# Matmuls in groups of two wide and two narrow, a fixed issue order on TensorE and a second column pair that runs one unit late

## The chip, the cores and the metric

The kernel runs on one core of a Trainium2 chip. The metric is device time in microseconds (us) of one execution. The kernel before takes 2563.12 us, the median of three runs (2562.52 to 2567.24).

## The reference: what is computed

A trunk of two pre-norm residual layers over 256 tokens of width 2048, each a token mixer followed by a gated feed-forward block, with a last RMSNorm. All inputs and outputs are float32.

```python
def ssd_mixer(u, w_in, conv_w, conv_b, dt_bias, a_log, d_skip, norm_w, w_out):   # layer 0
    z, xbc, dt_raw = split(u @ w_in)              # 2048 -> 4096 + 6144 + 64
    xbc = silu(causal_dwconv(xbc, conv_w, conv_b))
    y = ssd_chunked(...) + xh * d_skip            # 64 heads of 64, 8 groups, state 128
    yg = group_rms_norm(y * silu(z)) * norm_w
    return yg @ w_out                             # 4096 -> 2048

def short_conv_mixer(u, w_in, conv_w, w_out):     # layer 1
    bg, cg, h = split(u @ w_in, 3)                # 2048 -> 3 x 2048
    return (bg * causal_dwconv(cg * h, conv_w)) @ w_out

def conv_ffn(u, w_up, conv_w, conv_b, w_down):    # both layers
    g, v = split(causal_dwconv(u @ w_up, conv_w, conv_b), 2)    # 2048 -> 2 x 5632
    return (silu(g) * v) @ w_down                 # 5632 -> 2048

for i in range(2):
    x = x + mixer_i(rms_norm(x, mix_norm_w[i]))
    x = x + conv_ffn(rms_norm(x, ffn_norm_w[i]))
return rms_norm(x, final_norm_w)
```

## The kernel before

**Numbers in two parts.** Every large product is done with values of type float32r. A float32 operand is split into a high part (the value cast to float32r) and a low part (what the cast left out). A weight gives `wh` and `wl`; an activation gives the two halves of one tile `hl`, 256 columns (one per token) of high parts and 256 of low parts. The product of two such operands is taken as high times high, high times low and low times high. With the weight block as the stationary operand, `wh` meets both halves of `hl` in one matmul of 512 columns, which is called a wide product here (line 334 of the kernel before), and `wl` meets the high half in a matmul of 256 columns, a narrow one (line 335). Where the mixer of layer 0 needs the sum at once (`one=True`), the wide product is two narrow ones (lines 331 and 332).

**Units and streams.** A weight unit is 256 rows by 512 columns of a weight matrix. It is loaded by SyncE's queue into one of four `raw` buffers, ScalarE casts it to `wh` (line 287), and VectorE subtracts to get `wl` (line 288); `wh` and `wl` have four buffers each (`WB = 4`). A stream is one call of `stream`: 512 output columns, as two PSUM tiles of two banks (`pts`, the column pairs 0 and 1), accumulated over all units of the contraction (8 units for 2048 rows). For each unit it runs over the four column blocks `t` and over the two 128-row slices `k`. For each `(t, k)` it issues a wide product and then a narrow one, so a unit is eight wide and eight narrow products. `weight_unit` fetches up to `ahead` units beyond the one it returns; `stream` asks for three.

**Behind a stream.** `evac` takes each column pair out of PSUM. In the feed-forward block that is a copy on ScalarE (line 346), a sum and a product with the token's norm factor on VectorE (348, 357), a causal convolution over three positions (one ACTIVATE, line 368, and two SCALAR_TENSOR_TENSOR, line 370, for each of the two blocks), and then, in the gate's streams, a Silu (749), in the value's streams a product with the gate (755) and the split into a new `hl` (212, 213). A residual stream adds PSUM to `x` (698, 700). The PSUM pool `psm` has three such tiles, so that a stream's second tile is the one that the stream before it filled first.

**What sets the order.** The kernel is written in program order, and a scheduler with its own timeline then orders each engine's instructions; only those under `pin` keep their place. So on TensorE the products of two column pairs can change places where the scheduler expects a wait. SyncE's queue carries the weight loads.

**Stages.** The mixer of layer 0 comes first (eight groups of heads, with small matmuls between its streams, and its residual streams), then feed-forward block 0, the mixer of layer 1, and block 1. Block 1's second half differs: activations are stationary and weights move, so that each slice takes three wide products (lines 858 to 860), and the last norm is in token order.

Of the kernel before, what the change touches and what calls it, by code (L numbers as in the profile page):

```python
# [8 lines left out]
F32 = mybir.dt.float32  # L9
# [7 lines left out]
P = 128  # L17
# [22 lines left out]
def trunk_kernel(ctx, tc, a, out):  # L40
# [14 lines left out]
    dpool = ctx.enter_context(tc.tile_pool(name="dpool", bufs=1, space=DRAM))  # L55
    psm = ctx.enter_context(tc.tile_pool(name="psm", bufs=3, space=PSUM))
    psa = ctx.enter_context(tc.tile_pool(name="psa", bufs=2, space=PSUM))

    n_id = [0]

    def uid(s):
        n_id[0] += 1
        return f"{s}_{n_id[0]}"
# [244 lines left out]
    def stream(c0, hls, kcs, evac, one=False, before=None):  # L308

        pts = [psm.tile([P, 2, 512], F32, tag="main", name=uid("main")) for _ in range(2)]
        n = len(kcs)
        put = (lambda ins: ins) if before is None else pin
        for u in range(0, n, KU):
            order = [(t, k) for t in range(4) for k in range(KU)]
            if before is not None and u == 0:
                before(0)
                order.sort(key=lambda tk: tk[1])  # L320
            wh, wl = weight_unit(c0, kcs[u], WB - 1 if before is None else 0)
            for at, (t, k) in enumerate(order):
# [6 lines left out]
                first, last = i == 0, i == n - 1  # L329
                if one:  # L330
                    put(mm(o[:, 0:T], wh[:, k, lw], hl[:, 0:T], start=first, stop=False))  # L331
                    put(mm(o[:, 0:T], wh[:, k, lw], hl[:, T : 2 * T], start=False, stop=False))  # L332
                else:
                    put(mm(o, wh[:, k, lw], hl, start=first, stop=False))  # L334
                put(mm(o[:, 0:T], wl[:, k, lw], hl[:, 0:T], start=False, stop=last))  # L335
        if before is not None:
            before(n // KU)
        if taken[0] < len(plan):
            while len(units) < min(taken[0] + WB - 1, len(plan)):
                load_unit()  # L340
        for p in range(2):
            evac(p, pts[p])
# [345 lines left out]
            hls.append(h)  # L688
        return hls

    def residual_stream(hls, kcs, norm, nhl, nname, one=False):

        for cg in range(D // COLS):

            def evac(p, pt, cg=cg):
                m = 2 * cg + p
                x = xp[m]
                tt(out=x, in0=pt[:, :, 0:T], in1=x, op=ALU.add)
                if not one:
                    tt(out=x, in0=pt[:, :, T : 2 * T], in1=x, op=ALU.add)  # L700
# [39 lines left out]
    def ffn_part(l, part, hls, r):  # L740
        lo, hi = FPARTS[part]
        res = []
        for ch in range(lo, hi, 4):
            gs = []

            def evac_g(p, pt, ch=ch):
                k0 = ch + 2 * p
                y = conv(scaled(pt, r), W_FF, f"fw{l}", NF, k0, f"fb{l}", "g", gpool)
                act(y, y, AF.Silu)
                gs.append(y)  # L750

            def evac_v(p, pt, ch=ch):
                k0 = DFF // P + ch + 2 * p
                y = conv(scaled(pt, r), W_FF, f"fw{l}", NF, k0, f"fb{l}")
                tt(out=y, in0=gs[p], in1=y, op=ALU.mult)
# [11 lines left out]
    for part in range(2):  # L767
        hid = ffn_part(0, part, xhl, r)
        last = part == 1
        residual_stream(  # L770
            hid, range(*FPARTS[part]), norm if last else None, nhl,
            lambda m: ("mix", NKD + 2 * m),
        )


# [6 lines left out]
    for i in range(D // COLS):  # L782
# [21 lines left out]
    residual_stream(  # L804
        yhl, range(NKD), norm, nhl, lambda m: ("ffn", NKD + 2 * m)
    )


# [31 lines left out]
    for part in range(2):  # L840
# [3 lines left out]
        for cg in range(D // COLS):  # L844
# [6 lines left out]
            def products(c, u):  # L851
                wh, wl = held[u]
                for k in range(KU):
# [4 lines left out]
                    mm(pt[:, c, :], hi_, wh[:, k, :], start=(i == 0), stop=False)  # L858
                    mm(pt[:, c, :], hi_, wl[:, k, :], start=False, stop=False)  # L859
                    mm(pt[:, c, :], lo_, wh[:, k, :], start=False, stop=(i == n - 1))  # L860

            def evac(c):
                x = xtok[c][:, cols]
# [49 lines left out]
```

## Time and profile before

| | |
|---|---|
| median of three runs | 2563.12 us |
| the profiled execution | 2563.32 us |
| its span, first to last instruction | 2561.5 us |
| TensorE busy | 2544.6 us, 99% of the span |
| VectorE busy, ScalarE busy | 1790.2 us (70%), 1321.5 us (52%) |
| wide products of streams (line 334) | 5568 |
| narrow products of streams (331, 332, 335) | 768, 768, 6336 |
| wide products of block 1's last part (858 to 860) | 3 x 352 |
| read from HBM | 474 MB, 186 GB/s over the span |

The profiled execution lies 0.2 us above the median, and 1.8 us of it is outside the span. The ends of matmuls are modelled and overlap the next one's start: a wide product has a duration of 396 ns and starts about 230 ns before the next. So rates are read from start to start. "Busy 99%" says that TensorE had a matmul in flight nearly always, and not that it could go no faster.

### The profile page before, as it was taken

What the parts mean: (1) busy time and instruction counts of PE and PEld (TensorE: products, weight loads), DVE (VectorE), ACT (ScalarE), POOL (GpSimd) and SP (SyncE); (2) the same over time, 40 slices, a digit from 0 to 9 for tenths busy, and PEclk for the clock granted to TensorE, in tenths of its full rate; (3) what the DMA queues carried; (4) which work ended last, traced back from release to release, by engine and by line L of the source; (5) the groups of instructions that cost most, each with busy time, mean ns of one, the idle gap of its engine ahead of it and who ended that gap; (6) DMA issues with size and microseconds to landing.
All of it is one profiled execution on the core that took longest, in us unless ns stands there. A gap on an engine that the chain in (4) does not pass through costs nothing.

```text
span 2561.5 us, 38324 instructions
## 1 busy us (share of the span) xinstructions
PE 2544.6 (99%) x15101; PEld 2235.2 (87%) x15101; DVE 1790.2 (70%) x2601; ACT 1321.5 (52%) x1630; POOL 1.1 (0%) x8
## 2 busy tenths in 40 slices
PE   9999999999999999999999999999999999999998
PEld 9999998998888888888888888888888888888886
DVE  7888876788677776557776666666677774577765
ACT  5565643566555554345554444444555553455543
POOL 0000000000000000000000000000000000000000
PEclk9999999999999999999999999999999999999999
DMA  7666655665666665666665666666566666666664
GB/s 229 175 184 193 182 176 188 189 182 172 198 183 191 190 188 181 193 188 183 193 190 181 193 186 185 185 197 189 174 183 187 189 197 190 193 186 188 189 192 145
DMA packets 255737, 478.76 MB, mean 187 GB/s; under 512 B 17668, under 2 KB 29124, under 8 KB 255428
## 3 DMA queue, kind: packets, MB, share of 16 engines
q1 hardware_dynamic: 254643, 474.13, 61.3%
q8 instruction: 118, 1.93, 0.3%
q10 hardware_dynamic: 912, 2.18, 0.2%
q14 instruction: 64, 0.52, 0.1%
HBM read 474.09 MB, written 2.16 MB: 186 GB/s over the span
## 4 chain that ended last, share of the span: by engine, by line
PE 98%; DVE 1%; ACT 1%; DMA 0%; issue 0%; SPq 0%; DVEq 0%; ACTq 0%
PE main L334 50%; PE main L335 29%; PE main L331 3%; PE main L332 3%; PE main L858 3%; PE main L859 3%; PE main L860 3%; PE aux L649 1%; DVE wl L288 0%; PE aux L657 0%; DMA bias_bc<-in_ssd_dt_bias_dram 0%; PE aux L513 0%; PE aux L630 0%; DMA raw<-in_ssd_w_in_dram 0%; ACT wh L287 0%; PE aux L187 0%
## 5 line engine op out<-in xcount | busy, mean ns | idle before, releaser
L334 PE MATMUL main<-hl,wh 128*128 128x512 f32 x5568 | 1944.9, 396 | 0.2 <-DVE hl L218 0.2
L335 PE MATMUL main<-hl,wl 128*128 128x256 f32 x6336 | 1749.2, 281 | 1.8 <-DVE wl L288 1.8
L288 DVE TENSOR_TENSOR wl<-raw,wh 128x1024 fp32r<-128x1024 f32 (+1 forms) x881 | 1072.6, 1221 | 702.2 <-ACT wh L287 701.6
L287 ACT CAST wh<-raw 128x1024 fp32r<-128x1024 f32 (+1 forms) x881 | 920.8, 1048 | 1067.7 <-PE main L334 735.2
L334 PEld LDWEIGHTS main<-hl,wh 128*128 128x128 f32 x5568 | 1034.8, 188 | 236.7 <-issue 2.0
L335 PEld LDWEIGHTS main<-hl,wl 128*128 128x128 f32 x6336 | 1196.9, 189 | 17.6 <-DVE wl L288 2.7
L331 PE MATMUL main<-hl,wh 128*128 128x256 f32 x768 | 219.5, 287 | 2.5 <-DVE tp L354 1.3
L332 PE MATMUL main<-hl,wh 128*128 128x256 f32 x768 | 218.6, 285 | 0.0
L331 PEld LDWEIGHTS main<-hl,wh 128*128 128x128 f32 x768 | 148.2, 193 | 4.0 <-issue 2.0
L332 PEld LDWEIGHTS main<-hl,wh 128*128 128x128 f32 x768 | 148.3, 193 | 1.5 <-issue 1.1
L858 PE MATMUL main<-wh,hl 128*128 128x512 f32 x352 | 137.5, 391 | 0.8 <-DVE xtok L864 0.8
L859 PE MATMUL main<-wl,hl 128*128 128x512 f32 x352 | 137.4, 390 | 0.0
L860 PE MATMUL main<-wh,hl 128*128 128x512 f32 x352 | 137.0, 389 | 0.0
L370 DVE SCALAR_TENSOR_TENSOR tp<-tp,prm,tp 128x255 f32<-128x255 f32 x208 | 90.6, 477 | 0.0
L346 ACT COPY tp<-main 128x512 f32<-128x512 f32 x128 | 74.3, 580 | 26.0 <-PE main L335 26.0
L348 DVE TENSOR_TENSOR tp<-main,tp 128x512 f32<-128x512 f32 x128 | 87.4, 683 | 0.0
L858 PEld LDWEIGHTS main<-wh,hl 128*128 128x128 f32 x352 | 66.1, 188 | 15.3 <-DVE xtok L864 1.2
L860 PEld LDWEIGHTS main<-wh,hl 128*128 128x128 f32 x352 | 66.1, 188 | 14.2
L859 PEld LDWEIGHTS main<-wl,hl 128*128 128x128 f32 x352 | 66.1, 188 | 13.6
L370 DVE SCALAR_TENSOR_TENSOR g<-tp,prm,g 128x254 f32<-128x254 f32 (+1 forms) x176 | 74.6, 477 | 0.1
L368 ACT ACTIVATE g<-tp,prm,prm 128x256 f32<-128x256 f32 x88 | 48.2, 596 | 38.0 <-DVE tp L357 38.0
L357 DVE TENSOR_TENSOR tp<-tp,rrow 128x512 f32<-128x512 f32 x96 | 66.0, 688 | 1.8
(134 smaller groups left out, 966.9 us busy)
## 6 DMA issues: line engine op xcount, KB each, us to landing
raw<-in_ffn_w_up_dram SPq DMA_DIRECT2D x352, 512.0 KB, 3.7
raw<-in_ffn_w_down_dram SPq DMA_DIRECT2D x176, 512.0 KB, 4.1
raw<-in_ssd_w_in_dram SPq DMA_DIRECT2D x159, 512.0 KB, 4.5
raw<-in_sc_w_in_dram SPq DMA_DIRECT2D x96, 512.0 KB, 4.1
raw<-in_ssd_w_out_dram SPq DMA_DIRECT2D x64, 512.0 KB, 4.2
raw<-in_sc_w_out_dram SPq DMA_DIRECT2D x32, 512.0 KB, 4.2
cbc<-cs_d SPq DMA_DIRECT2D x32, 256.0 KB, 5.1
xt<-in_x_dram SPq DMA_DIRECT2D x8, 256.0 KB, 7.4
```

The source lines that it names most:

```text
L287: put(nc.scalar.copy(wh[:, ks, :], raw[:, ks, :]))
L288: put(tt(out=wl[:, ks, :], in0=raw[:, ks, :], in1=wh[:, ks, :].bitcast(F32), op=ALU.subtract,))
L331: put(mm(o[:, 0:T], wh[:, k, lw], hl[:, 0:T], start=first, stop=False))
L332: put(mm(o[:, 0:T], wh[:, k, lw], hl[:, T : 2 * T], start=False, stop=False))
L334: put(mm(o, wh[:, k, lw], hl, start=first, stop=False))
L335: put(mm(o[:, 0:T], wl[:, k, lw], hl[:, 0:T], start=False, stop=last))
L346: nc.scalar.copy(pb, pt[:, :, T : 2 * T])
L348: tt(out=s, in0=pt[:, :, 0:T], in1=pb, op=ALU.add)
L370: stt(out=y[:, j, d:T], in0=s[:, j, 0 : T - d], scalar=pcol(wname, (width - 1 - d) * nk + k0 + j), in1=y[:, j, d:T], op0=ALU.mult, op1=ALU ...
L858: mm(pt[:, c, :], hi_, wh[:, k, :], start=(i == 0), stop=False)
L859: mm(pt[:, c, :], hi_, wl[:, k, :], start=False, stop=False)
L860: mm(pt[:, c, :], lo_, wh[:, k, :], start=False, stop=(i == n - 1))
```

## The change

**The order within a column block.** In `stream`, the narrow products are held back: for each column block `t`, both slices' wide products come first and both narrow ones after (`low`, and the `elif` that calls it after slice `KU - 1`). This applies to all streams except the very first, whose order is written out (`before is not None`).

**A fixed issue order.** `follow` makes each matmul that goes through it depend on the one before it in program order, without a semaphore. It only takes from the scheduler the freedom to swap them.

**A late second pair.** `late_stream` takes the place of `stream` in everything behind the mixer of layer 0. In step `u` it issues column pair 0 for unit `u` and then column pair 1 for the unit before. A stream has one step more, its first step has only pair 0 and its last only pair 1. A unit's buffers are now held for one and a half steps, and `weight_unit` is asked for two units ahead in place of three. All its matmuls go through `follow`, and so do the three products of block 1's last part. `residual_stream` gets the stream function as its argument; its unused `one` is dropped.

No matmul, cast, load or PSUM access is added or removed, and no buffer count changes.

```diff
+    def follow(inst):
+        if last_main[0] is not None:
+            tc.add_manual_dep(
+                inst.ins, last_main[0],
+                mybir.DependencyInfo(
+                    mybir.DependencyClass.NoSync, mybir.DependencyReason.DATA
+                ),
+                reason="stream order",
+            )
+        last_main[0] = inst.ins.name
+        return inst
...
     def stream(c0, hls, kcs, evac, one=False, before=None):
+            def low(t, k):
+                i = u + k
+                put(mm(
+                    pts[t // 2][:, t % 2, 0:T], wl[:, k, t * P : (t + 1) * P],
+                    hls[i // 2][:, i % 2, 0:T], start=False, stop=(i == n - 1),
+                ))
+
             for at, (t, k) in enumerate(order):
...
                 else:
                     put(mm(o, wh[:, k, lw], hl, start=first, stop=False))
-                put(mm(o[:, 0:T], wl[:, k, lw], hl[:, 0:T], start=False, stop=last))
+                if before is not None:
+                    low(t, k)
+                elif k == KU - 1:
+                    for q in range(KU):
+                        low(t, q)
...
+    def late_stream(c0, hls, kcs, evac):
+        pts = [psm.tile([P, 2, 512], F32, tag="main", name=uid("main")) for _ in range(2)]
+        n = len(kcs)
+        held = {}
+
+        def half(p, u):
+            wh, wl = held[u]
+            for t in (2 * p, 2 * p + 1):
+                o = pts[p][:, t % 2, :]
+                lw = slice(t * P, (t + 1) * P)
+                part = [(u + k, k, hls[(u + k) // 2][:, (u + k) % 2, :]) for k in range(KU)]
+                for i, k, hl in part:
+                    follow(mm(o, wh[:, k, lw], hl, start=(i == 0), stop=False))
+                for i, k, hl in part:
+                    follow(mm(
+                        o[:, 0:T], wl[:, k, lw], hl[:, 0:T], start=False, stop=(i == n - 1)
+                    ))
+
+        for u in range(0, n + KU, KU):
+            if u < n:
+                held[u] = weight_unit(c0, kcs[u], WB - 2)
+                half(0, u)
+            if u:
+                half(1, u - KU)
+            while len(units) < min(taken[0] + WB - 1, len(plan)):
+                load_unit()
+        for p in range(2):
+            evac(p, pts[p])
...
-            stream(cg * COLS, hls, kcs, evac, one)
+            put(cg * COLS, hls, kcs, evac)
...
-            stream(ch * P, hls, range(NKD), evac_g)
-            stream(DFF + ch * P, hls, range(NKD), evac_v)
+            late_stream(ch * P, hls, range(NKD), evac_g)
+            late_stream(DFF + ch * P, hls, range(NKD), evac_v)
...
-            stream(n * D + i * COLS, xhl, range(NKD), ev)
+            late_stream(n * D + i * COLS, xhl, range(NKD), ev)
...
-                    mm(pt[:, c, :], hi_, wh[:, k, :], start=(i == 0), stop=False)
-                    mm(pt[:, c, :], hi_, wl[:, k, :], start=False, stop=False)
-                    mm(pt[:, c, :], lo_, wh[:, k, :], start=False, stop=(i == n - 1))
+                    follow(mm(pt[:, c, :], hi_, wh[:, k, :], start=(i == 0), stop=False))
+                    follow(mm(pt[:, c, :], hi_, wl[:, k, :], start=False, stop=False))
+                    follow(mm(pt[:, c, :], lo_, wh[:, k, :], start=False, stop=(i == n - 1)))
```

**TensorE, the first down-projection stream of block 0.** Before, in the third unit of the stream (its two PSUM tiles are `main_10281` and `main_10282`; `hl_8192` is the first pair of slices, `hl_8606` the third):

```order
L334 MATMUL main_10281<-hl_8606,wh_10229 128x512
L335 MATMUL main_10281<-hl_8606,wl_10230 128x256
L334 MATMUL main_10281<-hl_8606,wh_10229 128x512
L334 MATMUL main_10282<-hl_8192,wh_10185 128x512
L335 MATMUL main_10282<-hl_8192,wl_10186 128x256
```

The change, from the last unit of the stream before (`main_10071`, `main_10072`) to the first of this one; each row stands for the two slices, and equal rows in succession are two column blocks:

```order
L385 MATMUL main_10071<-hl_7752,wh_10171 128x512 x2
L387 MATMUL main_10071<-hl_7752,wl_10172 128x256 x2
L385 MATMUL main_10072<-hl_7742,wh_10149 128x512 x2
L387 MATMUL main_10072<-hl_7742,wl_10150 128x256 x2
L385 MATMUL main_10072<-hl_7742,wh_10149 128x512 x2
L387 MATMUL main_10072<-hl_7742,wl_10150 128x256 x2
L385 MATMUL main_10072<-hl_7752,wh_10171 128x512 x2
L387 MATMUL main_10072<-hl_7752,wl_10172 128x256 x2
L385 MATMUL main_10072<-hl_7752,wh_10171 128x512 x2
L387 MATMUL main_10072<-hl_7752,wl_10172 128x256 x2
L385 MATMUL main_10281<-hl_8192,wh_10193 128x512 x2
```

Before, wide and narrow alternate, but where the scheduler put off the second tile, a wide product follows a wide one; it did so for three units here, taking pair 0 through the first units before pair 1 began. In the whole program that happens 154 times. Now wide and narrow come in twos, pair 1 is a unit behind, and no product leaves its place.

**VectorE, at the end of a value stream** (`main_10071`; `wl` rows are weight units, the others the evacuation). Before:

```order
L348 TENSOR_TENSOR tp_10251<-main_10071,tp_10249 128x512
L357 TENSOR_TENSOR tp_10251<-tp_10251,rrow_7794 128x512
L288 TENSOR_TENSOR wl_10286<-raw_10283,wh_10285 128x1024
L370 SCALAR_TENSOR_TENSOR tp_10254<-tp_10251,prm_127,tp_10254 128x255 x2
L370 SCALAR_TENSOR_TENSOR tp_10254<-tp_10251,prm_126,tp_10254 128x254
L348 TENSOR_TENSOR tp_10267<-main_10072,tp_10265 128x512
L370 SCALAR_TENSOR_TENSOR tp_10254<-tp_10251,prm_126,tp_10254 128x254
L357 TENSOR_TENSOR tp_10267<-tp_10267,rrow_7794 128x512
L755 TENSOR_TENSOR tp_10254<-g_10050,tp_10254 128x512
L288 TENSOR_TENSOR wl_10308<-raw_10305,wh_10307 128x1024
```

The change:

```order
L406 TENSOR_TENSOR tp_10251<-main_10071,tp_10249 128x512
L415 TENSOR_TENSOR tp_10251<-tp_10251,rrow_7794 128x512
L303 TENSOR_TENSOR wl_10238<-raw_10235,wh_10237 128x1024
L428 SCALAR_TENSOR_TENSOR tp_10254<-tp_10251,prm_127,tp_10254 128x255 x2
L428 SCALAR_TENSOR_TENSOR tp_10254<-tp_10251,prm_126,tp_10254 128x254 x2
L303 TENSOR_TENSOR wl_10294<-raw_10291,wh_10293 128x1024
L406 TENSOR_TENSOR tp_10267<-main_10072,tp_10265 128x512
L812 TENSOR_TENSOR tp_10254<-g_10050,tp_10254 128x512
L415 TENSOR_TENSOR tp_10267<-tp_10267,rrow_7794 128x512
L303 TENSOR_TENSOR wl_10316<-raw_10313,wh_10315 128x1024
```

The second pair's sum (`tp_10267`) now comes one weight unit later, and the weight unit that stands first, `wl_10238`, is for the third unit of the next stream, where before it was the fourth (`wl_10286`).

More of the change, by code (lines that the diff above doesn't have):

```diff
@@ L328, in stream @@
                 lw = slice(t * P, (t + 1) * P)
-                first, last = i == 0, i == n - 1
+                first = i == 0
                 if one:
@@ L689, in ssd_gate, with residual_stream @@
         return hls
-    def residual_stream(hls, kcs, norm, nhl, nname, one=False):
+    def residual_stream(hls, kcs, norm, nhl, nname, put=stream):
         for cg in range(D // COLS):
@@ L698, in evac @@
                 tt(out=x, in0=pt[:, :, 0:T], in1=x, op=ALU.add)
-                if not one:
-                    tt(out=x, in0=pt[:, :, T : 2 * T], in1=x, op=ALU.add)
+                tt(out=x, in0=pt[:, :, T : 2 * T], in1=x, op=ALU.add)
                 if norm is not None:
@@ L771, in trunk_kernel @@
             hid, range(*FPARTS[part]), norm if last else None, nhl,
-            lambda m: ("mix", NKD + 2 * m),
+            lambda m: ("mix", NKD + 2 * m), late_stream,
         )
```

3 lines of the change are left out of this document (2 added, 1 removed).

## The prediction

> **What bounds the kernel now.** I read the page first, for the share of each engine, TensorE's granted clock in forty slices and the chain of work that ended last.
>
> ```profile
> span 2561.5 us, 38324 instructions
> PE 2544.6 (99%) x15101; PEld 2235.2 (87%) x15101; DVE 1790.2 (70%) x2601; ACT 1321.5 (52%) x1630; POOL 1.1 (0%) x8
> PEclk9999999999999999999999999999999999999999
> PE 98%; DVE 1%; ACT 1%; DMA 0%; issue 0%; SPq 0%; DVEq 0%; ACTq 0%
> L334 PE MATMUL main<-hl,wh 128*128 128x512 f32 x5568 | 1944.9, 396 | 0.2 <-DVE hl L218 0.2
> L335 PE MATMUL main<-hl,wl 128*128 128x256 f32 x6336 | 1749.2, 281 | 1.8 <-DVE wl L288 1.8
> ```
>
> TensorE is 98% of the chain, and the two lines that the change reorders are most of it. Next, the waits of TensorE:
>
> ```profile
> PE main L335 <- DVE wl L288: 1.8, 3, 1.4
> PE main L331 <- DVE tp L354: 1.3, 1, 1.3
> PE main L331 <- ACT hl L217: 1.2, 1, 1.2
> PE warm L96 <- DVE ones L91: 1.1, 1, 1.1
> PE main L858 <- DVE xtok L864: 0.8, 1, 0.8
> PE aux L194 <- DVE nacc L680: 0.3, 1, 0.3
> PE main L334 <- DVE hl L218: 0.2, 1, 0.2
> ```
>
> They add up to 6.7 us in the whole program. So almost no time is waiting, and the span is the sum of the matmuls' spacings. A change of order can move the time in two ways: by another spacing, or by a wait that is not there now.
>
> So I read the spacing, from start to start in the timeline. Wide and narrow alternate in two regular rhythms. The first two rows below are the ends of a stretch with 44 wide-narrow pairs between their starts, the other two the ends of one with 6:
>
> ```profile
> 1000.06 0.39 PE L334 MATMUL main<-hl,wh 128*128 128x512 f32 x1
> ...
> 1015.31 0.39 PE L334 MATMUL main<-hl,wh 128*128 128x512 f32 x1
> ...
> 1038.94 0.40 PE L334 MATMUL main<-hl,wh 128*128 128x512 f32 x1
> ...
> 1041.06 0.40 PE L334 MATMUL main<-hl,wh 128*128 128x512 f32 x1
> ```
>
> 15.25 us over 44 is 346.6 ns a pair; 2.12 us over 6 is 353.3 ns. Runs of one width alone stand in the mixer (narrow, 36 spacings) and in block 1's last part (wide, 9 spacings, and 13 in another stretch):
>
> ```profile
> 299.74 0.28 PE L335 MATMUL main<-hl,wl 128*128 128x256 f32 x1
> ...
> 304.06 0.28 PE L335 MATMUL main<-hl,wl 128*128 128x256 f32 x1
> ...
> 2106.28 0.39 PE L858 MATMUL main<-wh,hl 128*128 128x512 f32 x1
> ...
> 2108.32 0.39 PE L858 MATMUL main<-wh,hl 128*128 128x512 f32 x1
> ...
> 2499.80 0.39 PE L859 MATMUL main<-wl,hl 128*128 128x512 f32 x1
> ...
> 2502.78 0.39 PE L860 MATMUL main<-wh,hl 128*128 128x512 f32 x1
> ```
>
> A narrow product among narrow ones takes 4.32 / 36 = 120.0 ns. A wide one among wide ones takes 2.04 / 9 = 226.7 ns at its fastest, and 2.98 / 13 = 229.2 ns in the slower stretch. 226.7 + 120.0 = 346.7: the fast rhythm of the pairs is just the sum of the two kinds alone, and the slow rhythm is 6.7 ns more. The mean lies between:
>
> ```profile
> L334 PE MATMUL main<-hl,wh 128*128 128x512 f32 x2851 | 993.8, 396 | 0.0
> L187 PE MATMUL aux<-dg,ones 128*128 128x128 f32 x8 | 1.2, 274 | 0.0
> L194 PE MATMUL aux<-ones,nacc 128*128 128x1 f32 x8 | 1.0, 229 | 0.0
> ```
>
> These are groups of the 1000 us from 700 on. Less the 2.2 us of the small matmuls, 997.8 / 2851 = 350.0 ns a pair, or 3.4 ns over the fast rhythm: about half of the pairs run in each. That surplus is what a new order can act on: 5568 pairs x 3.4 ns = 18.9 us.
>
> **The change part by part.** *Two wide, two narrow.* A column block's four products hold the same work as two pairs, 2784 such quads in all. The trace has hardly one quad in this order, so its price is bounded. From below: the sum of the kinds alone, 2 x 346.6 = 693.2 ns, which takes off the whole 18.9 us. From above: the few doubles that the scheduler made,
>
> ```profile
> 1019.53 0.63 PE L334 MATMUL main<-hl,wh 128*128 128x512 f32 x2
> 1020.00 0.28 PE L335 MATMUL main<-hl,wl 128*128 128x256 f32 x1
> ...
> 1023.88 0.40 PE L335 MATMUL main<-hl,wl 128*128 128x256 f32 x2
> 1024.12 0.39 PE L334 MATMUL main<-hl,wh 128*128 128x512 f32 x1
> ```
>
> with 0.47 us for two wide and 0.24 us for two narrow, 710 ns together against 700.0 now: +10 ns x 2784 = +27.8 us. These rows are rounded to 0.01 us and lie in a slow stretch. A steady slow rhythm, 706.7 ns, would cost 6.7 x 2784 = 18.7 us. I take a value between, nearer to the lower end, by the row that a repeated order resembles most: a run of one width never shows the 6.7 ns (0 for narrow, 0 to 2.5 for wide), and the alternation does, so I put the surplus on the changes of width. A pair has two of them for its 3.4 ns. A quad also has two, where two pairs have four. So half of the surplus goes: 3.4 x 2784 = 9.5 us.
>
> [...]
>
> *The three-narrow streams* (`one`) keep a run of narrow products only: 120.0 ns each in any order, nothing.
>
> *Fixed order.* It adds no semaphore. What it could save is TensorE's waiting behind the mixer, of which the rows above can hold no more than L858's 0.8 and L334's 0.2 and a little of L335: under 1 us, taken as 0. What it takes away is the scheduler's means to cover a wait by a swap, so I look at the two things that pair 0 and pair 1 wait for.
>
> *PSUM.* With pairs at 350.0 ns a half unit is 8 / 2 x 350.0 = 1.4 us. After pair 0 of a stream is complete, its last two halves of pair 1 and the next stream's first two halves of pair 0 are issued before its tile is written again: 4 x 1.4 = 5.6 us. The evacuation reads it with a copy and one sum (groups of the same 1000 us, here and below):
>
> ```profile
> L346 ACT COPY tp<-main 128x512 f32<-128x512 f32 x65 | 37.7, 580 | 14.9 <-PE main L335 14.9
> L348 DVE TENSOR_TENSOR tp<-main,tp 128x512 f32<-128x512 f32 x64 | 43.7, 683 | 0.0
> ```
>
> 0.58 + 0.68 = 1.26 us. It is hidden, with 4.3 us to spare for what is queued ahead.
>
> *Weights.* A buffer that a unit frees at the end of step u is refilled for step u + 3, where before a whole three units lay between. The lead falls from 3 x 2.8 = 8.4 us to 5.6 us. Cast and subtraction need 1.05 + 1.22 = 2.27 us:
>
> ```profile
> L287 ACT CAST wh<-raw 128x1024 fp32r<-128x1024 f32 x356 | 372.7, 1050 | 457.7 <-PE main L334 406.4 <-issue 46.2 <-ACT wh L287 2.9
> L288 DVE TENSOR_TENSOR wl<-raw,wh 128x1024 fp32r<-128x1024 f32 x357 | 435.9, 1224 | 331.1 <-ACT wh L287 331.1
> L357 DVE TENSOR_TENSOR tp<-tp,rrow 128x512 f32<-128x512 f32 x50 | 34.4, 688 | 1.0
> L370 DVE SCALAR_TENSOR_TENSOR tp<-tp,prm,tp 128x254 f32<-128x254 f32 x56 | 25.5, 476 | 0.0
> L755 DVE TENSOR_TENSOR tp<-g,tp 128x512 f32<-128x512 f32 x22 | 15.0, 683 | 0.0
> L213 DVE TENSOR_TENSOR hl<-tp,hl 128x512 fp32r<-128x512 f32 x28 | 19.1, 683 | 0.0
> ...
> 1033.39 1.23 DVE L288 TENSOR_TENSOR wl<-raw,wh 128x1024 fp32r<-128x1024 f32 x1 [1.60 <-ACT wh L287]
> ```
>
> That leaves 3.3 us. VectorE is fullest behind a value stream: each pair costs 0.683 + 0.688 + 4 x 0.476 + 0.683 + 0.683 = 4.64 us, and in the order of the change some five weight units (6.1 us) stand among the two pairs' 9.3 us. That is 15.4 us of work in five steps of 2.8 = 14.0 us: it falls behind by 1.4 us at most, under the 3.3 us of slack. Cost 0; away from an evacuation VectorE is idle for 1.60 us before each weight unit (the last row), so the lag does not pile up. If the cover were gone, 22 value streams (11 groups in each of two blocks) would stop TensorE by up to 1.4 us each, 31 us.
>
> *Transfers* keep their number and order on SyncE's queue; only the subtraction that frees a `raw` buffer comes up to one step later. Taken as 0.
>
> Sum: 2563.3 (the profiled execution, 0.2 above the median, a difference I let go) - 9.5 = 2553.8, say **2554 us**.
>
> **The rivals.** *All of the surplus goes* (chance 0.24). The quad, repeated undisturbed over hundreds of units, settles in the fast rhythm: 2563.3 - 18.9 = 2544 us. For it: a rhythm holds for tens of pairs, and wide products alone keep the fast one too, so an order that repeats may stay in it. Against: nothing here shows which one it would choose.
>
> *Order does not matter* (0.21). The surplus belongs to each matmul's place in time, not to its neighbour. For it: the doubles take about what their neighbours take. The quad stays at 700 ns, 2563 us, give or take 4.
>
> *The quad locks in the slow rhythm* (0.17). Each quad takes 706.7 ns, from the first unit behind the mixer on: 2563.3 + 18.7 = 2582 us. It decides if more than three quarters of the quads are slow, since half of the pairs are today. For it: the doubles above give no gain, and the slow rhythm still runs after them, at 1038.94. Against: no run of one width shows 6.7 ns.
>
> *Weights come late* (0.06). The slack of 3.3 us is used up by semaphores and queues, and the in-order stream stops behind every value stream: 2554 + 31 = 2585 us.
>
> **How the numbers follow.** The forecast has 0.32, the others as given. A measurement of this kernel can tell about 0.2%, 5 us, from no change. Forecast and full gain are faster: 0.56. The third is the same: 0.21. The last two are slower: 0.23. The range reaches from the full gain, with 4 us for waits and for small matmuls that no longer disturb, to the slow lock less 2: 2540 to 2580. It leaves out the late weights and a part of the slow lock. The likeliest case alone spans 2549 to 2558.
>
> **What would show each step.** In the changed kernel's timeline, the start-to-start time of a quad: 693 for the full gain, 696 to 697 for the forecast, 700 for no effect, 707 for the slow lock, read over a long window as time per wide product (348 ns in the forecast). In the waits, TensorE for `wl` or `wh`: some 2 us as now if the slack holds, tens of us with many entries if it does not; TensorE for `tp` or `x` by the evacuation would show that PSUM is not hidden. The number of busy PE instructions stays at 15101. The forecast is wrong if the quads' spacing is the same and the time moves, or if the spacing changes outside 693 to 707, for then the rhythm is set by something that this trace does not show.

## The result, and the profile after

| | time, us (median, lowest to highest) | profiled span, us | ratio to before (95%) |
|---|---|---|---|
| before | 2562.82 (2562.39 to 2567.24) | 2561.5 | |
| after | 2550.65 (2550.55 to 2550.94) | 2548.9 | 0.9949 (0.9932 to 0.9966) |

The kernel became faster by 12.2 us; the forecast was 9.5 us. The page of the changed kernel has the same shape as before (its head, and the shares of the chain):

```profile
span 2548.9 us, 38320 instructions
PE 2531.7 (99%) x15101; PEld 2227.2 (87%) x15101; DVE 1795.7 (70%) x2601; ACT 1317.4 (52%) x1622; POOL 1.1 (0%) x8
...
PE 98%; DMA 1%; DVE 1%; ACT 0%; SPq 0%; issue 0%; DVEq 0%
```

Two rows of TensorE's waits (us in all, times, longest), on the sums of the evacuation and on the weights:

```profile
PE main L354 <- DVE tp L412: 1.3, 1, 1.3
...
PE main L340 <- DVE wl L303: 1.1, 1, 1.1
```

All entries of this view add up to 6.6 us, against 6.7 before, and TensorE's busy time went down by 12.9 us with the same 15101 instructions. So the time came out of the spacing of the matmuls. These are the wide products of the changed kernel in the 1000 us from 700 on (the second row is the end of the mixer):

```profile
L385 PE MATMUL main<-hl,wh 128*128 128x512 f32 x2843 | 892.9, 395 | 0.0
L357 PE MATMUL main<-hl,wh 128*128 128x512 f32 x24 | 7.5, 395 | 0.0
```

and this is its timeline over five quads, from the start of the first to the start of the sixth:

```profile
1499.85 0.63 PE L385 MATMUL main<-hl,wh 128*128 128x512 f32 x2
1500.32 0.39 PE L387 MATMUL main<-hl,wl 128*128 128x256 f32 x2
...
1503.33 0.62 PE L385 MATMUL main<-hl,wh 128*128 128x512 f32 x2
```

997.8 / 2867 = 348.0 ns per wide product with its narrow one, where before it was 350.0; and 3.48 us / 5 = 696 ns a quad. Where in the program the time went shows in one line's first and last start, the copy of the norm's row: its first stands where feed-forward block 0 begins, its last where feed-forward block 1 begins.

```profile
L399 ACT COPY rrow<-aux x3: 372/373/373, 731.9 to 1832.3; 128x256 f32<-128x256 f32 x3
```

is before, and after the change the same line reads

```profile
L457 ACT COPY rrow<-aux x3: 373/373/373, 728.3 to 1822.3; 128x256 f32<-128x256 f32 x3
```

3.6 us are gone by the first mark, 10.0 by the last, 12.6 at the end of the span. The change acts about evenly over the program, in the mixer too, where `late_stream` is not used. But 1.1 of the 3.6 us can't be the grouping's: they are there before the first wide product. The 299th matmul, a narrow one behind the same wait, starts at 46.33 us before and at 45.20 us after:

```profile
46.33 0.35 PE L331 MATMUL main<-hl,wh 128*128 128x256 f32 x1 [1.28 <-DVE tp L354]
```

```profile
45.20 0.35 PE L354 MATMUL main<-hl,wh 128*128 128x256 f32 x1 [1.28 <-DVE tp L412]
```

What makes the start shorter was not traced.

### The profile page after: what moved, and what is told of

The parts are those of the page before. It is cut to its first block, busy times and chain, and to the rows that moved or that the text cites. A ratio compares the mean times of both kernels' runs of the same rounds, so it can differ in the third digit from the quotient of the medians.

```text
span 2548.9 us, 38320 instructions
## 1 busy us (share of the span) xinstructions
PE 2531.7 (99%) x15101; PEld 2227.2 (87%) x15101; DVE 1795.7 (70%) x2601; ACT 1317.4 (52%) x1622; POOL 1.1 (0%) x8
## 4 chain that ended last, share of the span: by engine, by line
PE 98%; DMA 1%; DVE 1%; ACT 0%; SPq 0%; issue 0%; DVEq 0%
PE main L385 41%; PE main L387 21%; PE main L357 9%; PE main L340 8%; PE main L354 4%; PE main L355 4%; PE main L915 3%; PE main L916 3%; PE main L917 3%; PE aux L707 1%; DMA raw<-in_ssd_w_in_dram 0%; DMA cbc<-cs_d 0%; PE aux L715 0%; PE aux L571 0%; PE aux L688 0%; PE aux L202 0%
## 5 line engine op out<-in xcount | busy, mean ns | idle before, releaser
L385 PE MATMUL main<-hl,wh 128*128 128x512 f32 x4544 | 1427.5, 395 | 0.0
L387 PEld LDWEIGHTS main<-hl,wl 128*128 128x128 f32 x4544 | 853.4, 188 | 201.0
L387 PE MATMUL main<-hl,wl 128*128 128x256 f32 x4544 | 893.6, 278 | 0.0
L385 PEld LDWEIGHTS main<-hl,wh 128*128 128x128 f32 x4544 | 691.6, 189 | 0.1
L340 PE MATMUL main<-hl,wl 128*128 128x256 f32 x1792 | 362.0, 282 | 1.3 <-DVE wl L303 1.1
L340 PEld LDWEIGHTS main<-hl,wl 128*128 128x128 f32 x1792 | 311.0, 190 | 47.7 <-issue 3.3
L357 PE MATMUL main<-hl,wh 128*128 128x512 f32 x1024 | 321.4, 397 | 0.8 <-DVE hl L233 0.8
L354 PE MATMUL main<-hl,wh 128*128 128x256 f32 x768 | 204.3, 286 | 2.5 <-DVE tp L412 1.3
L355 PE MATMUL main<-hl,wh 128*128 128x256 f32 x768 | 203.3, 285 | 0.3
L357 PEld LDWEIGHTS main<-hl,wh 128*128 128x128 f32 x1024 | 157.5, 189 | 3.2 <-DVE hl L233 1.0
L354 PEld LDWEIGHTS main<-hl,wh 128*128 128x128 f32 x768 | 147.9, 193 | 3.5 <-issue 2.1
L355 PEld LDWEIGHTS main<-hl,wh 128*128 128x128 f32 x768 | 147.9, 193 | 1.1 <-DVE hl L233 0.7
```

What stands on the lines that cost most here:

```text
L340: put(mm(pts[t // 2][:, t % 2, 0:T], wl[:, k, t * P : (t + 1) * P], hls[i // 2][:, i % 2, 0:T], start=False, stop=(i == n - 1),))
L385: follow(mm(o, wh[:, k, lw], hl, start=(i == 0), stop=False))
L387: follow(mm(o[:, 0:T], wl[:, k, lw], hl[:, 0:T], start=False, stop=(i == n - 1)))
```

## Experiments

**Theories.** *Mine* (the forecast): each change of width costs 3.4 ns per pair of changes, so fewer changes cost less, and neither the fixed order nor the late pair matters. *Rivals*: the gain is the fixed order's or the late pair's; or the spacing hangs on something else than the number of changes.

### Grouping alone

The kernel before, with the narrow products held back as in the new `stream`; no `follow`, no `late_stream`:

```diff
-                put(mm(o[:, 0:T], wl[:, k, lw], hl[:, 0:T], start=False, stop=last))
+                if before is not None:
+                    low(t, k)
+                elif k == KU - 1:
+                    for q in range(KU):
+                        low(t, q)
```

> Grouping alone: the kernel before with two wide, two narrow products in every column block, the scheduler free to swap, no late pair. Theory (the surplus belongs to changes of width): nearly all quads are in the new order (2632 against 2715 in the changed kernel), so a quad takes about 697 ns and the time is 2551 to 2553 us, all of the changed kernel's gain but for the fifty or so broken groups. Rival (the fixed order makes the gain, because swaps throw the rhythm): half or more of the gain is lost, 2557 to 2563 us, and quads between swaps take unequal times.

Measured: 2551.03 us, 0.9952 (0.9940 to 0.9965), where the kernel before took 2563.49 us in the same set of runs. Its wide products from 700 to 1700:

```profile
L342 PE MATMUL main<-hl,wh 128*128 128x512 f32 x2867 | 899.4, 395 | 0.0
```

2867, as many as in the changed kernel. The grouping alone gives the whole gain, to within 0.4 us.

### Fixed order and late pair alone

The changed kernel, with wide and narrow alternating everywhere:

```diff
                 for i, k, hl in part:
                     follow(mm(o, wh[:, k, lw], hl, start=(i == 0), stop=False))
-                for i, k, hl in part:
                     follow(mm(
                         o[:, 0:T], wl[:, k, lw], hl[:, 0:T], start=False, stop=(i == n - 1)
```

and in `stream` the lines of `low` are taken back as well.

> The late pair and the fixed order alone: wide and narrow alternate as before. Theory: each pair still has two changes of width, so the mean stays at about 350 ns a pair and the time at 2560 to 2566 us. Rival (undisturbed order lets the pairs keep the fast rhythm): 346.7 ns a pair behind the mixer, 4544 x 3.4 ns = 15 us less, about 2548 us. Third: the undisturbed pairs keep the slow rhythm, 353.3 ns, 2578 us.

Measured: 2569.43 us (2564.47 to 2573.74), 1.0023 (1.0014 to 1.0032): slower than before. Its wide products in the 1000 us from 700 on:

```profile
L373 PE MATMUL main<-hl,wh 128*128 128x512 f32 x2806 | 987.1, 397 | 0.0
L349 PE MATMUL main<-hl,wh 128*128 128x512 f32 x33 | 11.6, 398 | 0.0
```

and TensorE's longest entry in its waits:

```profile
PE main L350 <- DVE wl L303: 2.0, 3, 1.4
```

The waits are the same size as before, so the slack for PSUM and weights held here too. What grew is the spacing: 997.8 / 2839 = 351.5 ns a pair. With pairs in this order, the slow rhythm (353.3) is met more often than the fast one; why the late pair or the fixed order tilts it that way was not tested. In the grouped kernel these two parts move the time by less than can be measured.

### Fewer changes of width

The changed kernel with four wide and four narrow products a column pair, and another with eight and eight a step. The core of the first (the second also splits `half` into a wide and a narrow part, called for both pairs):

```diff
-                elif k == KU - 1:
-                    for q in range(KU):
-                        low(t, q)
+                elif k == KU - 1 and t % 2 == 1:
+                    for s in (t - 1, t):
+                        for q in range(KU):
+                            low(s, q)
```

> As the changed kernel, with four wide and four narrow products for each column pair (both its blocks). Theory (about 3.4 ns for each two changes of width): eight products take 4 x 346.6 + 3.4 = 1390 ns where the changed kernel takes 2 x 696.7 = 1393.4, 3.4 x 1392 = 4.7 us less, 2546 us. Rival (the surplus is a matter of the phase in which a repeated order locks): anything from 1386.7 to 1400 ns, 2541 to 2560 us, with no relation to the number of changes.

> As the changed kernel, with eight wide and eight narrow products in a step (both column pairs together). Theory: sixteen products take 8 x 346.6 + 3.4 = 2776 ns, a further 2.4 us or so less than with four and four, about 2544 us, near the floor of 2563.3 - 18.9 = 2544. Rival (phase): 2773 to 2800 ns, 2541 to 2560 us. The subtraction of the low part has more time, so no new wait for it.

Measured: 2562.61 us, 0.9997 (0.9988 to 1.0005), and 2561.7 us, 0.9992 (0.9983 to 1.0001). No gain is left. Two octets of the first in the timeline (four wide, four narrow, then the next wide ones):

```profile
1500.95 1.09 PE L386 MATMUL main<-hl,wh 128*128 128x512 f32 x4
1501.88 0.63 PE L391 MATMUL main<-hl,wl 128*128 128x256 f32 x4
1502.35 1.09 PE L386 MATMUL main<-hl,wh 128*128 128x512 f32 x4
```

and the sixteen products of a step of the second:

```profile
1500.51 2.00 PE L384 MATMUL main<-hl,wh 128*128 128x512 f32 x8
1502.36 1.12 PE L394 MATMUL main<-hl,wl 128*128 128x256 f32 x8
1503.31 0.86 PE L384 MATMUL main<-hl,wh 128*128 128x512 f32 x3
```

1.40 us an octet against 1.386 for four times 346.6; 2.80 us for sixteen, against 2.773. By my theory these would have been 1390 and 2776 ns: it falls. Over the window, the time above 346.6 per wide product is 3.4 ns for pairs, 1.4 for quads, 3.8 for octets (997.8 / 2848 = 350.4) and 2.3 for sixteens (997.8 / 2860 = 348.9). That does not go by the number of changes. The two starts in the last view also show where it sits: eight wide products take 1.85 us, 231 ns each, and eight narrow ones 0.95 us, 119. The wide ones behind narrow ones are long, against 226.7 ns in a run of wide ones alone.

### Where the operands lie

**A new theory.** In the changed kernel most quads take 697 ns, but 128 of them mostly 693. I lined up the matmul records of the trace with the addresses of the tiles in the program: the 693s are those whose moving operand `hl` lies at 64 modulo 128 bytes within a partition (tiles of the second `hl` pool, `hlpool2`, which serve the first four units of each down-projection stream of block 0), while all others have both operands, `hl` and the stationary `wh` or `wl`, at 0. In octets and sixteens the same tiles stand out (1387 against 1401 to 1406, 2773 against 2793). So the spacing may hang on the place of the two operands relative to each other. Four kernels test it: the changed one with all of its first `hl` pool 64 bytes further (an unused tile of 16 numbers ahead of the pool, one of 112 behind it, so that nothing else changes its place modulo 512); with the weights moved instead; the kernel before with `hl` moved; and the changed one with those few tiles at 64 put at 0. The first:

```diff
+    pada = ctx.enter_context(tc.tile_pool(name="pada", bufs=1))
+    pada.tile([P, 16], F32, tag="pada", name="pada")
     hlpool = ctx.enter_context(tc.tile_pool(name="hlpool", bufs=16))
+    padb = ctx.enter_context(tc.tile_pool(name="padb", bufs=1))
+    padb.tile([P, 112], F32, tag="padb", name="padb")
```

The second has the same two pools around `wpool`, the third is the first's edit on the kernel before, the fourth has a tile of 16 numbers ahead of `hlpool2`.

> The changed kernel with every hl tile moved by 64 bytes (an unused pad before the hl pool and one behind it, so that all weight tiles stay at multiples of 512 bytes). In the changed kernel the 128 quads whose hl lies at an odd multiple of 64 bytes take 693.3 ns, the sum of the kinds alone, and the others 696.7. Theory (the surplus is a collision of the moving operand's reads with the weight load's, set by their relative address): all quads take 693 to 694 ns, 2650 x 3.4 = 9.0 us less; the last part's wide products, whose stationary operand is hl, all take 229 in place of 226.7 ns, 670 x 2.2 = 1.5 us more; together 2543 us. Rival (those 128 quads are fast because of their place behind the first units of a stream, not because of the address): 2551 us, quads at 696.7.

> The changed kernel with the wh and wl tiles moved by 64 bytes and the hl tiles left. Theory (only the relative address counts): quads with hl at 0 take 693 to 694 ns as if hl had been moved, and the quads with the four hl tiles at 64 take 696.7; 2542 to 2545 us. Rival (the moving operand's own address counts): quads at 0 stay at 696.7 ns, 2550 to 2552 us. For the last part's wide products (now moving operand at 64) theory says 229 ns where hl is at 0 and 226.7 where it is at 64.

> The kernel before (wide and narrow alternating) with every hl tile moved by 64 bytes. In the kernel before, the pairs whose hl lies at 64 take 353.3 ns nearly all, the others 350.4 in the mean. Theory (address and order together set the rhythm): all pairs take about 353 ns, 4814 x 2.6 = 12.5 us more, and the last part 1.5 us more, 2577 us: the same move of 64 bytes that speeds up quads slows down pairs. Rival (64 bytes apart is free of collisions in any order): pairs at 346.7 ns, 2546 us.

> The changed kernel with only the four tiles of the second hl pool moved, to multiples of 512 bytes like all others. Theory: the 128 quads that used them go from 693.3 to 696.7 ns (0.4 us more), and the 384 wide products of the last part that have them as stationary operand go from 229 to 226.7 ns (0.9 us less): 2550 us, to be read in the trace alone. Rival (place in the stream): both keep their spacing.

Measured:

| edit | us | ratio (95%) | ns per wide product, 700 to 1700 |
|---|---|---|---|
| quads, `hl` + 64 | 2534.25 | 0.9884 (0.9870 to 0.9897) | 345.3 |
| quads, weights + 64 | 2536.78 | 0.9893 (0.9878 to 0.9908) | 346.7 |
| before (pairs), `hl` + 64 | 2568.12 | 1.0015 (1.0006 to 1.0024) | 351.0 |
| quads, second `hl` pool at 0 | 2549.92 (one run) | | 348.0 |

Moving `hl` by sixteen unused numbers takes 16.4 us off the changed kernel, more than the change itself does. The first kernel's wide products in the window:

```profile
L389 PE MATMUL main<-hl,wh 128*128 128x512 f32 x2888 | 897.6, 392 | 0.0
L361 PE MATMUL main<-hl,wh 128*128 128x512 f32 x2 | 0.6, 390 | 0.0
```

Its timeline at the ends of 38 spacings of narrow products alone, in the mixer, and of 15 quads:

```profile
300.05 0.28 PE L358 MATMUL main<-hl,wh 128*128 128x256 f32 x1
...
304.52 0.28 PE L358 MATMUL main<-hl,wh 128*128 128x256 f32 x1
...
1560.00 0.62 PE L389 MATMUL main<-hl,wh 128*128 128x512 f32 x2
...
1570.35 0.62 PE L389 MATMUL main<-hl,wh 128*128 128x512 f32 x2
```

4.47 us / 38 is 117.6 ns a narrow product, where before it was 120.0, and 10.35 us / 15 is 690 ns a quad. Its stage marks:

```profile
L461 ACT COPY rrow<-aux x3: 373/373/375, 720.5 to 1805.6; 128x256 f32<-128x256 f32 x3
```

By the marks 7.8 us go in the mixer: 2.4 ns on each of its 3 x 768 products of the three-narrow streams make 5.5, and the quads there the rest. 16.7 us are gone by the start of block 1. Block 1 as a whole then takes 0.5 us more than in the changed kernel: its streams are shorter and its last part is longer (below).

The kernel before is the sharper test. Its window:

```profile
L338 PE MATMUL main<-hl,wh 128*128 128x512 f32 x2843 | 993.7, 395 | 0.0
```

A pair takes 351.0 ns here against 350.0 in the kernel before: the move that helps quads does not help pairs. The 0.15% of the whole kernel is a sum of gains and losses, as its stage marks show:

```profile
L403 ACT COPY rrow<-aux x3: 372/373/373, 727.5 to 1830.5; 128x256 f32<-128x256 f32 x3
```

Against the kernel before, 4.4 us are gone by the first mark (in the mixer with its runs of narrow products), the stretch between the marks, which holds streams of pairs alone, is 2.6 us longer, and block 1 is 6.2 us longer, 5.2 of them by the records in its last part. So most of the loss is not the pairs'. That pairs became slower at all is 1 ns from one trace each, and the runs of the kernel before scatter by 5 us, which is about 1 ns a pair. The window refutes the rival that distance alone sets the price, which put pairs at 346.7, and it refutes my theory's sizes as well, which put pairs at 353 and the kernel at 2577 us. The fourth kernel agrees with the theory in the place it is about: the records of the 128 quads went from 693 to mostly 696 to 698 ns, and those wide products of the last part that have the same tiles as stationary operand from 229.0 to 226.8.

The second kernel tells whether each operand's own place counts or the place of one relative to the other. Its weights are at 64, most of its `hl` at 0, but the `hl` of the second pool at 64 too. The latter are the very quads that took 693 ns in the changed kernel. The first two rows are the ends of a stretch of nine quads with `hl` at 0, the other two of one of twelve with both operands at 64:

```profile
1025.53 0.62 PE L389 MATMUL main<-hl,wh 128*128 128x512 f32 x2
...
1031.77 0.63 PE L389 MATMUL main<-hl,wh 128*128 128x512 f32 x2
...
1033.18 0.62 PE L389 MATMUL main<-hl,wh 128*128 128x512 f32 x2
...
1041.54 0.63 PE L389 MATMUL main<-hl,wh 128*128 128x512 f32 x2
```

6.24 / 9 = 693.3 ns against 8.36 / 12 = 696.7. With both operands moved the quads are back where they are with neither moved, as the theory has it; a gain from each operand's own place would have stayed. Over all quads of this trace it is 693.6 and 698.9 in the mean, and 692 and 701 in the kernel with weights in two places (below). What stands is that the spacing hangs on the order and on the place of the two operands relative to each other.

The last part has the roles turned round: the weights move and `hl` stands. There the move costs. 18 spacings of wide products, in the kernel before:

```profile
2139.71 0.39 PE L858 MATMUL main<-wh,hl 128*128 128x512 f32 x1
...
2143.79 0.39 PE L858 MATMUL main<-wh,hl 128*128 128x512 f32 x1
```

and in the changed one with `hl` 64 bytes on:

```profile
2139.61 0.39 PE L920 MATMUL main<-wl,hl 128*128 128x512 f32 x1
...
2143.81 0.39 PE L920 MATMUL main<-wl,hl 128*128 128x512 f32 x1
```

4.08 / 18 = 226.7 ns against 4.20 / 18 = 233.3.

### How far, and a version for both parts

Four more, all with quads. *Weights in two places*: weight tiles are 128 bytes longer, and are used from byte 64 on in the streams and from byte 0 in the last part, so that each part has what was best for it. *Wide mixer*: `hl` + 64, and the mixer's three-narrow streams written as wide and narrow, since 345.3 ns is less than three times 117.6; the same sum is computed, with one more copy and one more addition in the evacuation. And `hl` moved by 32 and by 128 bytes.

```diff
+        at = 0 if i in last_down else 16
+        def weights(tag):
+            t = wpool.tile([P, KU * COLS + 32], F32R, tag=tag, name=uid(tag))
+            return t[:, at : at + KU * COLS].rearrange("p (k n) -> p k n", k=KU)
```

```diff
-            y = conv(scaled(pt, r0, True), W_SSD, "ssdw", NCX, g * 4 + 2 * p, "ssdb", "xs", xspool)
+            y = conv(scaled(pt, r0), W_SSD, "ssdw", NCX, g * 4 + 2 * p, "ssdb", "xs", xspool)
...
-        stream(DI + g * GC, xhl, range(NKD), evac, True)
+        stream(DI + g * GC, xhl, range(NKD), evac)
```

(the second also in the streams of B and C). For 32 and 128 bytes the unused tiles have 8 and 120, or 32 and 96 numbers.

> The changed kernel with the weight tiles 128 bytes longer, used from byte 64 on in all streams and from byte 0 in the last part, where activations are the stationary operand. Theory (each part has its own good pair of addresses: 64 apart for streams, both at multiples of 128 for the last part): quads and narrow runs as with the weights moved by 64 everywhere (693 to 695 and 116.6 ns), and the last part's wide products at 227 to 229 ns in place of 231 to 232, 2.9 us less than that run, 2534 us. Rival (the last part was slowed by something else): 2537 us.

> The changed kernel with all hl tiles at 64, and the mixer's streams that took three narrow products now with a wide and a narrow one as all others (but the first stream), which needs a copy and a sum more for each column pair behind them. Theory: three narrow products take 3 x 118.3 = 355 ns and half a quad 346, 9 ns x 704 = 6.3 us less than with the hl tiles moved alone, 2528 us. Rival (VectorE, over 80% busy in the mixer, gets 22 sums of 0.68 us more and TensorE waits for it): 2534 us or more, with waits of TensorE for wl or the small matmuls' inputs.

> The changed kernel with the hl tiles moved by 32 bytes in place of 64 (the last four stay at 64). Theory (what counts is in which 64-byte half of 128 bytes a row begins): as not moved, quads 696.7 and narrow ones 120 ns, 2550 us. Rival (the distance counts by degrees): quads between 692 and 696 ns, 2538 to 2548 us.

> The changed kernel with the hl tiles moved by 128 bytes: the same pads, the same order, only another place. Theory (address modulo 128): as the changed kernel, quads 696.7, narrow ones 120 ns, 2550 us. Rival (the pads, or another multiple, made the gain): 2534 to 2545 us.

| edit | us | ratio (95%) | ns per wide product, 700 to 1700 |
|---|---|---|---|
| weights in two places | 2532.93 | 0.9882 (0.9868 to 0.9895) | 346.0 |
| `hl` + 64, wide mixer | 2547.14 | 0.9936 (0.9922 to 0.9950) | |
| `hl` + 32 | 2541.06 (one run) | | 346.5 |
| `hl` + 128 | 2552.97 (one run) | | 348.2 |

*Weights in two places* is the fastest of all, with the first `hl` move 1.3 us behind it, which the intervals do not separate; both beat the kernel before by 1.2% and the changed one by 0.6 to 0.7%. But not as expected: the last part did not get its 226.7 ns back,

```profile
2139.79 0.39 PE L929 MATMUL main<-wh,hl 128*128 128x512 f32 x1
...
2143.95 0.39 PE L929 MATMUL main<-wh,hl 128*128 128x512 f32 x1
```

4.16 / 18 = 231.1, and the records give 231 ns in the mean for those of these products whose operands are both at 0 modulo 128, where the expectation had the time of before. The tiles' length had changed, and with it their place modulo 512; whether that is the reason was not tested.

*`hl` + 128* gave quads of 695 to 699 ns, 697 in the mean, as the theory has it, and yet long products in the last part by the records (233 in the mean where both operands are at 0 modulo 128; 4.12 / 18 = 228.9 in the stretch below, which is part of that):

```profile
2139.73 0.39 PE L919 MATMUL main<-wh,hl 128*128 128x512 f32 x1
...
2143.85 0.39 PE L919 MATMUL main<-wh,hl 128*128 128x512 f32 x1
```

So "modulo 128 bytes" is not the whole rule there. *`hl` + 32* worked nearly like 64 for the quads (693 ns most often), so "which half of 128 bytes" is not the rule either. And in the kernel with `hl` + 64 the quads with `hl` in the second pool take 693 ns most often, those with `hl` in the moved pool 687 to 693 (690 in the mean), though both lie at 64 modulo 128. A finer scan of places was not run; the rule stays open.

*The wide mixer* lost 12.9 us. TensorE now waits for VectorE in the mixer. Two of its waits:

```profile
PE main L361 <- DVE tp L410: 4.6, 2, 3.7
PE aux L206 <- DVE dg L198: 2.8, 1, 2.8
```

and the stretch from 64 to 640 us (its length, then the busy time of PE, its weight loads, DVE and ACT):

```profile
64.00:640.00 576.00, 565.18 (x3388) 487.76 (x3388) 476.44 (x900) 321.02 (x400) 0.00 (x0) 0.99 0.60 183
```

The same stretch with `hl` + 64 alone:

```profile
64.00:640.00 576.00, 573.82 (x4078) 524.05 (x4078) 472.96 (x891) 321.88 (x394) 0.00 (x0) 1.00 0.62 186
```

TensorE is idle for 8.6 us more in this stretch, and VectorE was busy for 82% of it without the added work. The stage marks of the wide mixer,

```profile
L461 ACT COPY rrow<-aux x3: 372/372/372, 733.8 to 1818.9; 128x256 f32<-128x256 f32 x3
```

are 13.3 us late at the first, against 720.5. With 1.8 us more between 640 and 740 us, TensorE's idle time grew by about 10.5 us up to there. The granted clock is the other part. It is at half in two stretches, and each begins within one of the two long waits above (the 0.50 is the clock's share of full speed; the next figures are the DMA share and GB/s):

```profile
302.60:309.40 6.80, 5.64 (x17) 4.86 (x18) 6.73 (x15) 4.23 (x8) 0.00 (x0) 0.50 0.23 82
637.10:647.30 10.20, 5.99 (x18) 5.02 (x19) 5.02 (x18) 1.70 (x4) 0.00 (x0) 0.50 0.27 99
```

With `hl` + 64 alone it is 1.00 in both. In the two stretches TensorE was busy for 5.64 + 5.99 = 11.6 us. By estimate, from the share of 0.50, half of that was the price, 5.8 us. 10.5 + 5.8 = 16.3, less the 13.3 measured, leaves 3.0 us gained by the new products, where 6.3 had been expected; that difference was not traced.

## Why the prediction was right, and where it was not

- **What bounds the kernel: right.** The span is the sum of the matmuls' spacings. Every kernel above but the wide mixer moved with the spacing alone; TensorE's waits add up to 6.6 to 8.6 us in all of them, and to 18.3 in the wide mixer.
- **The sum: nearly right.** Forecast 9.5 us, measured 12.2. The term is 5568 wide products by half of 3.4 ns, 1.7. Measured is 2.0 (350.0 to 348.0). Over the 4544 products behind the mixer this makes 9.1 us, and the marks show 12.6 - 3.6 = 9.0. In the mixer 1024 products by 2.0 make 2.0 us, and the marks show 3.6, of which 1.1 are there before the first wide product; the 0.5 left were not traced further. So of the 12.2 us about 11 belong to the term of the forecast, and 1.1 to the start, of which the forecast says nothing.
- **"I put the surplus on the changes of width ... So half of the surplus goes": wrong in its reason.** This is the step that failed. The quad came out at 696 ns, where the forecast's 696.6 was to be, but octets and sixteens, with still fewer changes, have the surplus back. The halving was a guess between two bounds that landed on the value by luck; a price for each change of width is not what the runs show. In its place they show that the spacing depends on the order together with the place of the two operands in memory (quads: about 697 ns with both at 0 or both at 64, 693 or less with one of them moved), which no view of the profile before shows, because all its tiles had the same place but those few, and views do not show places. Why the quad at that place costs 3 ns and not 0 or 7 is not explained.
- **"The sum of the kinds alone" as the bound from below: wrong.** 2 x 346.6 = 693.2 ns was taken for what a quad must have. With `hl` 64 bytes on, quads take 690 in the timeline, narrow products alone 117.6. The fastest of the rhythms seen was a rate of that layout, not of the engine.
- **The fixed order at 0: right in the grouped kernel.** With grouping alone the time is the same. In alternating order, however, the fixed order and the late pair together cost 0.23%, by the spacing of pairs: "it adds no semaphore" is no proof that it is free.
- **PSUM and weights: right.** TensorE's waits for `wl` and `tp` are of the size they had, 1.1 and 1.3 us, in a kernel where pair 1 is a unit late. VectorE did its two-part evacuation and the weight units between them in time:

```profile
1197.46 0.69 DVE L406 TENSOR_TENSOR tp<-main,tp 128x512 f32<-128x512 f32 x1
1199.09 1.23 DVE L303 TENSOR_TENSOR wl<-raw,wh 128x1024 fp32r<-128x1024 f32 x1 [0.21 <-ACT wh L302]
...
1210.23 1.23 DVE L303 TENSOR_TENSOR wl<-raw,wh 128x1024 fp32r<-128x1024 f32 x1
```

In this evacuation it still has a gap of 0.21 us ahead of a weight unit, and at its end none, but nobody waits.
- **The rivals.** "Order does not matter" falls with the first experiment: the order of the same products is worth 12.5 us (2563.49 to 2551.03), or about 11 without the shorter start. "All of the surplus goes" needs 693 ns a quad, and only the 128 quads with `hl` at 64 had it, most of them. The slow lock and the late weights did not come.

## What to carry to other kernels

In this kernel, where TensorE is 98% of the chain and waits for under 7 us, the order of its products was a knob worth 0.5% (2562.82 to 2550.65 us), and the place of its two operands in SBUF was another, here the larger one (16 us of 2550 for 64 bytes of padding). Both have to be measured, and together: the move that helped quads (696 to 690 ns) did not help pairs (350.0 to 351.0) and made the products with activations as the stationary operand longer (226.7 to 233.3), and longer groups (2562.61 and 2561.7 us) undid what groups of two had gained. Before a regular rhythm is called a floor, move one operand by 64 bytes and look again.

## What the runs showed of the hardware

- With float32 operands rounded for TensorE (`fp32r`), the same wide product, among its kind, took from 226.7 ns (last part of the kernel before, `hl` at 0) to 233.3 (`hl` 64 bytes on), and the same narrow product 120.0 or 117.6, by where the tiles lie; the granted clock was 0.998 or 0.999 in the profiled runs of all kernels here but the wide mixer (0.994).
- A move of either operand by 64 bytes has nearly the same effect on the kernel (2534.25 and 2536.78 us), and with both at 64 the quads are back at 696.7 ns, which points to their relative place. That their reads collide, as the theory of the first move had it, no view shows; what the runs show is the spacing by place. The distance modulo 128 bytes is not the whole rule: with `hl` 128 bytes on, the quads take 697 ns in the mean as in the changed kernel, but products of the last part with both operands at 0 take 233 ns by the records, and with 32 bytes the quads take 693 most often.
- The excess of long groups lies in the wide products that follow narrow ones: in the kernel with sixteens, the records give 233, 236, 228, 232, 231, 227, 227, 227 ns for the eight wide ones in turn, and 114, 119, then six times 120 for the narrow ones. So in that kernel, with both operands at 0, it took five products for the wide spacing to settle near the 226.7 of a long run, and the groups of two of the changed kernel do not get there: both wide products of its quads take 233 ns by the records.
- In the wide mixer two stretches of 6.8 and 10.2 us at half the granted clock begin within waits of 3.7 and 2.8 us for VectorE; in the kernel without these waits the clock is 1.00 there. One trace suggests by this that its waits cost more than their own length, by estimate 5.8 us beside 10.5 of idle time; it was not tested.
